# Retention states of both directions formed a head ahead, scores two steps ahead, five side banks

## The chip, the cores and the metric

The kernel runs on one core of a Trainium2 chip. The metric is the device time of one execution in microseconds (us), median of several runs. A core has a matrix engine (TensorE, in the profile PE, with its weight loads shown apart as PEld), a vector engine (VectorE, DVE), an engine for activations (ScalarE, ACT), a general one (GpSimd, POOL) and a queue that issues transfers (SyncE, SP). TensorE writes to PSUM, an accumulator of eight banks of 128 x 512 fp32 numbers.

## The reference, cut to what matters

The model is one layer of a diffusion transformer over 1024 latent tokens and 256 context tokens: a combined projection, retention and differential attention side by side, an output projection, and a gated feed-forward part. The change touches retention alone. It has four heads of 128 x 128, and it works in chunks of 128 tokens, in both directions over the sequence:

```python
def step(S, inp):                       # for each of 8 chunks; S starts from the context's 2 chunks
    qc, kc, vc = inp
    scores = einsum('bhid,bhjd->bhij', qc, kc) * intra
    o = einsum('bhij,bhje->bhie', scores, vc) + einsum('bhid,bhde->bhie', qc * q_dec[..., None], S)
    S = S * c_dec[:, None, None] + einsum('bhjd,bhje->bhde', kc * k_dec[..., None], vc)
    return S, o
...
for d in range(2):                      # forward, and backward over the flipped sequence
    o_l, _ = retention_chunked(ql, kl, vl, log_gamma[d], s_c)
    ret_lat = ret_lat + head_group_norm(orient(o_l), gn_g[d])
y_ret_lat = silu(rg_l) * ret_lat
```

So the state S of a chunk needs the state of the chunk before it, and each output needs one state of each direction.

## The kernel before, in words

Projections are done in fp32 split into a high and a low part, three matmuls of 512 columns for each product (`passes`, L129 to L131). A projection block is eight accumulations into a PSUM bank; each takes eight products (`KD`), 24 matmuls. `natural` (L387) and `transposed` (L442) run such blocks, and after each product they call `tick` (L376), which adds a rate to a counter and runs as many parts of a generator as the counter has whole numbers. Retention hangs on these ticks as side work. All of its matmuls are 128 x 128 in plain fp32, and the profile records two for each.

The parts around the change, in program order:

- The block of k (`transposed`, L695), which also writes k, transposed back, to DRAM.
- The block of the gate (`natural`, L698; 64 ticks). Beside it runs `states_before` (L318): the backward states of all four heads, 36 parts, one chunk each. GpSimd scales k (`kscale`, L229), TensorE forms k times v (`pub`, L334), VectorE adds it to the decayed state (`state_step`, L234), into `Sb`.
- The block of q (`transposed`, L701; 64 ticks), then six of the eight accumulations of the attention's q (L704; 48 ticks). Beside both runs `outputs` (L351) at 1.2 parts for each tick, from a counter of -12. A step is one chunk of one head; there are 32 steps, and each has three parts: the load and the score of the next step with the transpose of three steps back; the step's output; and the forward state's update with the gate of the step before.
- The last two accumulations of that block (L823), in whose course the attention begins.

In a step, `Step` has GpSimd scale q for both directions (`qq`, L256); `score` (L270) forms `pc` on TensorE and VectorE multiplies it with the decays (`sc`, L274); `output` (L276) accumulates `po` from four matmuls, ScalarE copies it to `o` (L282, two buffers) and sums its squares (L286), VectorE adds the norm's constant (`ss`, L114) and GpSimd raises to the power -1/2 (`ss`, L115); `update` (L289) forms `puf` and the next forward state `Sf`; `gate` (L295) multiplies with the norm on VectorE (L297) and adds and gates on GpSimd (`y`, L299, L300); `turn` (L302) transposes on TensorE (`pyt`, L304) and splits on ScalarE and VectorE (`yr`, L309, L310). The first forward state of a head comes from the context (`first_state`, L258; `context_keys`, L345, scaled by L348).

PSUM: the projections rotate through five banks (`mm_tiles`, L162), all side work through three (`pst`, L158, tag `tr`).

The order of the instructions of each engine is fixed when the kernel is built, by the framework: program order is the priority, but an instruction that by the framework's own estimate is not ready yet lets later ones go first. In the trace a product's three matmuls are therefore parted by side work at places. On the chip each engine then runs its list strictly in order.

Of the kernel before, what the change touches and what calls it, by code (L numbers as in the profile page):

```python
# [72 lines left out]
def kernel(  # L73
# [78 lines left out]
    with ExitStack() as p1:  # L152
# [8 lines left out]
        ps_b = psx.enter_context(tc.tile_pool(name="psb1", bufs=3, space=PSUM))  # L161
        mm_tiles = itertools.cycle([ps_b] * 3 + [ps_a] * 2)  # L162

        def mm_tile(name):
            return next(mm_tiles).tile([P, 512], F32, name=name, tag="mm")
# [52 lines left out]
        def load_kvg(h, g, nm, n, bufs=4):  # L218
            kvg = rt.tile([P, 2 if nm == "c" else 3, 2, P], F32, name=f"kvg{nm}", bufs=bufs)
            nc.sync.dma_start(out=kvg[:, :n], in_=kvg_d[g][:, :n, :, h * P : (h + 1) * P])  # L220
            return kvg
# [6 lines left out]

        def kscale(k1, h, d):  # L229
            kk = rt.tile([P, P], F32, name=f"ks{d}")  # L230
            nc.gpsimd.tensor_scalar(out=kk, in0=k1, scalar1=kd[:, h, d : d + 1], scalar2=0.0, op0=ALU.mult, op1=ALU.add)
            return kk

        def state_step(dst, prev, pu, h, d):  # L234
            if prev is None:
                nc.vector.tensor_copy(dst, pu)
            else:
                nc.vector.scalar_tensor_tensor(out=dst, in0=prev, scalar=cd[:, d * H + h : d * H + h + 1], in1=pu, op0=ALU.mult, op1=ALU.add)

        class Step:  # L240
            def __init__(self, n):
                self.h, self.t = divmod(n, NT)
                h, t = self.h, self.t
                if t % 2 == 0:
# [3 lines left out]
                    steps["pair"] = (qk, load_kvg(h, t // 2 + 1, "f", 3))  # L248
                qk, kvg = steps["pair"]
                self.qT, self.kT = (qk[:, i, t % 2 * P : (t % 2 + 1) * P] for i in range(2))  # L250
                self.kn, self.v, self.sg = (kvg[:, i, t % 2, :] for i in range(3))
                self.S = None
# [3 lines left out]
                nc.gpsimd.tensor_tensor(out=self.qq, in0=self.qT.unsqueeze(1).to_broadcast([P, 2, P]), in1=qd[:, h], op=ALU.mult)  # L256

            def first_state(self):  # L258
                ctx, kk = steps["ctx"]
                pu = pst.tile([P, NTC, P], F32, name="puc", tag="tr")  # L260
                for c in range(NTC):
                    mm(pu[:, c, :], kk[:, c, :], ctx[:, 1, c, :], start=True, stop=True)
# [55 lines left out]
        def states_before():  # L318
# [4 lines left out]
            for h, c in seq + [(None, None)]:  # L323
# [18 lines left out]
                if c is not None:  # L342
                    yield
# [7 lines left out]
        def outputs():  # L351
            n_steps = H * NT
            for n in range(-2, n_steps + 4):
# [12 lines left out]
                if new and (n + 1) % NT == 0:  # L366
                    steps[n + 1].first_state()
# [1011 lines left out]
```

## Time and profile before

| | |
|---|---|
| median of 3 runs | 1448.55 us (1448.17 to 1450.31) |
| the profiled execution | 1441.0 us, its span 1439.2 us |
| mean granted TensorE clock in it | 0.992 |
| PE, PEld busy | 1379.9 us (96%), 1141.9 us (79%) |
| DVE, ACT, POOL busy | 1003.8 us (70%), 732.4 us (51%), 340.8 us (24%) |
| chain that ended last | PE 66%, DVE 8%, DMA 5%, POOL 3% |

Durations come from the profiled execution. A line of the profile names the engine, the line of the kernel, the tiles (what is written, an arrow, what is read), the shapes and the count. Behind the bar stand busy time and the mean of one instruction in ns, then the idle time of the engine just ahead of it with what ended it. A matmul's end is modelled, so the start of the next one says more than its recorded duration. A waiting weight load (PEld) is the first sign of TensorE standing still.

### The profile page before, as it was taken

The numbers are of one execution on the slowest core, as the hardware profiler recorded it, in microseconds if no ns is written. First come the engines' busy times: TensorE is split into PE (matmuls) and PEld (weight loads), VectorE is DVE, ScalarE is ACT, GpSimd is POOL, SyncE is SP. The second block draws the span as 40 slices with busy tenths as digits, with TensorE's granted clock in tenths as the row PEclk, the third lists the DMA queues.
The fourth block names the chain that finished last, engine by engine and source line by source line (L and its number), as shares of the span: only waits on it lengthen the run. The fifth ranks groups of instructions, "written<-read, shape, count | busy, mean of one in ns | idle before, by whom it ended". The sixth has DMA issues, their size and how long they took to land.

```text
span 1439.2 us, 19420 instructions
## 1 busy us (share of the span) xinstructions
PE 1379.9 (96%) x6924; PEld 1141.9 (79%) x6924; DVE 1003.8 (70%) x1493; ACT 732.4 (51%) x1394; POOL 340.8 (24%) x451
## 2 busy tenths in 40 slices
PE   6999999999899899999999899999999999999996
PEld 2678787887777789999888677888888888888885
DVE  3565655333677598888346888878777777998457
ACT  3535512322456688998224655555555545455533
POOL 1210000022787323431002253322223230000001
PEclk9999999999999999999999999999999999999999
DMA  8557655466455767480511123223222224953224
GB/s 332 199 194 240 219 196 190 137 193 195 134 173 164 208 156 164 121 143 1 220 62 78 59 104 118 108 110 110 92 87 93 110 110 174 391 206 102 101 95 176
DMA packets 107673, 218.30 MB, mean 152 GB/s; under 512 B 8948, under 2 KB 47348, under 8 KB 106680
## 3 DMA queue, kind: packets, MB, share of 16 engines
q1 hardware_dynamic: 99448, 192.14, 38.3%
q0 software_dynamic: 8128, 24.91, 7.7%
q8 instruction: 55, 0.90, 0.3%
q14 instruction: 42, 0.34, 0.1%
HBM read 159.61 MB, written 57.41 MB: 151 GB/s over the span
## 4 chain that ended last, share of the span: by engine, by line
PE 66%; DVE 8%; DMA 5%; POOL 3%; issue 3%; ACT 3%; SPq 0%; POOLq 0%; DVEq 0%; ACTq 0%
PE chain L129 5%; PE pv L760 5%; PE chain L130 5%; PE pA L728 5%; PE chain L131 5%; PE c L131 4%; PE c L129 4%; PE c L130 4%; PE third L130 2%; PE third L129 2%; PE third L131 2%; DMA W<-w_down 2%; PE pt L748 2%; PE pn L130 2%; PE pn L131 2%
## 5 line engine op out<-in xcount | busy, mean ns | idle before, releaser
L129 PE MATMUL chain<-T,whi 128*128 128x512 f32 x264 | 103.8, 394 | 4.9 <-ACT T L941 3.3
L129 PE MATMUL pl<-hT,whi 128*128 128x512 f32 x256 | 107.1, 419 | 0.0
L130 PE MATMUL chain<-T,whi 128*128 128x512 f32 x264 | 103.2, 391 | 0.0
L131 PE MATMUL chain<-T,wlo 128*128 128x512 f32 x264 | 102.6, 390 | 0.0
L131 PE MATMUL pl<-hT,wlo 128*128 128x512 f32 x256 | 100.5, 393 | 0.0
L130 PE MATMUL pl<-hT,whi 128*128 128x512 f32 x256 | 100.5, 393 | 0.0
L731 DVE TENSOR_REDUCE mt<-pA 128x1 f32<-128x1280 f32 x64 | 95.3, 1490 | 3.3 <-PE pA L728 1.5
L728 PE MATMUL pA<-ks,qhl 128*128 128x512 f32 (+1 forms) x384 | 91.6, 375 | 4.7 <-ACT p L735 4.7
L1024 POOL TENSOR_TENSOR cmb<-wrb 128x512 f32<-128x512 f32 x22 | 36.2, 1647 | 243.2 <-DMA wrb<-w_up 141.3
L131 PE MATMUL c<-whi,ghl 128*128 128x512 f32 x232 | 90.4, 390 | 0.2 <-DVE ghl L1183 0.2
L130 PE MATMUL c<-wlo,ghl 128*128 128x512 f32 x232 | 90.3, 389 | 0.0
L129 PE MATMUL c<-whi,ghl 128*128 128x512 f32 x232 | 90.2, 389 | 0.0
L115 POOL TENSOR_TENSOR sm<-sm,mhalf 128x1 f32<-128x1 f32 x26 | 16.1, 621 | 304.7 <-DVE sm L114 301.4
L735 ACT ACTIVATE p<-pA,mt 128x1280 f32<-128x1280 f32 x64 | 85.5, 1336 | 4.6 <-DVE mt L731 4.5
L894 ACT CAST whi<-cmb 128x512 fp32r<-128x512 f32 x66 | 41.0, 622 | 83.5 <-PE chain L130 63.7
L728 PEld LDWEIGHTS pA<-ks,qhl 128*128 128x128 f32 x384 | 68.9, 193 | 17.5 <-ACT p L735 5.8
L129 PE MATMUL pn<-whi,hT 128*128 128x512 f32 x192 | 79.1, 412 | 0.0
L760 PE MATMUL pv<-va,aT 128*128 128x128 f32 x640 | 77.0, 275 | 0.1
L131 PE MATMUL pn<-whi,hT 128*128 128x512 f32 x192 | 75.9, 398 | 0.5 <-DVE hT L540 0.5
L130 PE MATMUL pn<-wlo,hT 128*128 128x512 f32 x192 | 76.1, 396 | 0.0
L895 DVE TENSOR_TENSOR wlo<-cmb,whi 128x512 fp32r<-128x512 f32 x66 | 60.7, 922 | 20.2 <-ACT whi L894 20.2
L760 PEld LDWEIGHTS pv<-va,aT 128*128 128x128 f32 x640 | 74.0, 192 | 0.7 <-DVE yT L789 0.3
(301 smaller groups left out, 3884.1 us busy)
## 6 DMA issues: line engine op xcount, KB each, us to landing
wm<-w_mod SPq DMA_DIRECT2D x32, 512.0 KB, 4.4
raw<-w_in SPq DMA_DIRECT2D x28, 512.0 KB, 4.4
wra<-w_up SPq DMA_DIRECT2D x24, 512.0 KB, 3.2
wrb<-w_up SPq DMA_DIRECT2D x24, 512.0 KB, 3.5
W<-w_down SPq DMA_DIRECT2D x44, 256.0 KB, 6.4
ad<-s SPq DMA_DIRECT2D x20, 512.0 KB, 3.4
wra<-ad SPq DMA_DIRECT2D x20, 512.0 KB, 3.2
wrb<-ad SPq DMA_DIRECT2D x18, 512.0 KB, 3.3
```

The lines of the kernel that those rows point to most:

```text
L115: nc.gpsimd.tensor_tensor(out=out_ap, in0=out_ap, in1=mhalf[:, :n], op=ALU.pow)
L129: mm(ps, lh, rh, start=first, stop=False, skip_group_check=more)
L130: mm(ps, lh, rl, start=False, stop=False, skip_group_check=more)
L131: mm(ps, ll, rh, start=False, stop=last, skip_group_check=more)
L728: mm(self.pa[m][:, c0:c1], self.q[:, i, m, qs], self.k[:, m, c0:c1], start=(i == 0), stop=(i == 1))
L731: nc.vector.tensor_reduce(out=self.mt[:, m : m + 1], in_=self.pa[m][:, :LK], axis=AX.X, op=ALU.min)
L735: nc.scalar.activation(self.p[m], self.pa[m][:, :LK], AF.Exp, scale=-1.0, bias=self.mt[:, m : m + 1], accum_out=self.s[:, m : m + 1])
L748: nc.tensor.transpose(self.pt[g][:, i, :], self.p[0][:, (4 * g + i) * P : (4 * g + i + 1) * P], ident)
L760: mm(self.pv, self.aT[:, c, :], self.v[:, c, :], start=(c == 0), stop=(c == NKT - 1))
L894: nc.scalar.copy(hi, src)
L895: nc.vector.tensor_tensor(out=lo, in0=src, in1=r32(hi), op=ALU.subtract)
L1024: nc.gpsimd.tensor_tensor(out=s1, in0=b1, in1=b2, op=ALU.add)
```

## The change

States of both directions are formed by one generator, `states(h)`: pairs of chunks are loaded (`kvs`, four buffers), GpSimd scales both chunks of a pair in one instruction (`ks`, 128 x 256), and forward and backward pairs alternate; a head has 18 parts as before (9 for each direction). The states of heads 0 and 1 are formed beside the gate's block, those of heads 2 and 3 within `outputs`, from steps 8 and 16 on, three parts in each of the first six steps of the head. All states lie in `S0` and `S1`, with buffers for two heads. `update`, `first_state`, `context_keys` and their tiles are gone. A step loads v and gate alone (`kvo`) and q and k.

The score is formed two steps ahead of the output instead of one (`lead = 2`; `qq` and `sc` get three buffers). Parts of a step: score with transpose; output with gate; in steps outside 8 to 23 an empty part. The rate is 1.5 for each tick from -21. The norm's constant is added on GpSimd (`tensor_scalar`), just ahead of the power.

From the gate's block on, the banks are dealt anew: three for the projections, five for the side work.

```diff
-        ps_b = psx.enter_context(tc.tile_pool(name="psb1", bufs=3, space=PSUM))
-        mm_tiles = itertools.cycle([ps_b] * 3 + [ps_a] * 2)
+        psbS = psx.enter_context(ExitStack())
+        ps_b = psbS.enter_context(tc.tile_pool(name="psb1", bufs=3, space=PSUM))
+        banks = dict(mm=itertools.cycle([ps_b] * 3 + [ps_a] * 2))
...
+        def tr_tile(shape, name):
+            return next(banks["tr"]).tile(shape, F32, name=name, tag="tr")
...
+        def load_kv(h, g, nm, s0, bufs):
+            kv = rt.tile([P, 2, 2, P], F32, name=nm, bufs=bufs)
+            nc.sync.dma_start(out=kv, in_=kvg_d[g][:, s0 : s0 + 2, :, h * P : (h + 1) * P])
+            return kv
...
-                    steps["pair"] = (qk, load_kvg(h, t // 2 + 1, "f", 3))
+                    steps["pair"] = (qk, load_kv(h, t // 2 + 1, "kvo", 1, 3))
...
-                if t < NT - 1:
-                    self.kk = kscale(self.kn, h, 0)
-                self.qq = rt.tile([P, 2, P], F32, name="qq")
+                self.qq = rt.tile([P, 2, P], F32, name="qq", bufs=3)
...
-                self.sc = rt.tile([P, 2, P], F32, name="sc")
+                self.sc = rt.tile([P, 2, P], F32, name="sc", bufs=3)
...
-                for d, Sd in enumerate((self.S, Sbs[self.h][:, self.t, :])):
+                for d in range(2):
                     mm(po[:, d, :], self.sc[:, d, :], self.v, start=True, stop=False)
-                    mm(po[:, d, :], self.qq[:, d, :], Sd, start=False, stop=True)
+                    mm(po[:, d, :], self.qq[:, d, :], before[self.h][d][:, self.t, :], start=False, stop=True)
...
-                rsqrt(self.ss, self.ss, 1.0, GN_EPS * P, 2)
+                nc.gpsimd.tensor_scalar(out=self.ss, in0=self.ss, scalar1=1.0, scalar2=GN_EPS * P, op0=ALU.mult, op1=ALU.add)
+                nc.gpsimd.tensor_tensor(out=self.ss, in0=self.ss, in1=mhalf[:, :2], op=ALU.pow)
...
+        def states(h):
+            seq = [(0, 0, (0, 1)), (1, 0, (1, 0))]
+            for g in range(1, 5):
+                seq += [(0, g, (0, 1) if g < 4 else (0,)), (1, 5 - g, (1, 0) if g < 4 else (1,))]
+            before[h] = [rt.tile([P, NT, P], F32, name=f"S{d}") for d in range(2)]
...
+            def loaded(i):
+                d, g, cs = seq[i]
+                kv = ctx if i == 1 else load_kv(h, g, "kvs", 0, 4)
+                ks = rt.tile([P, 2, P], F32, name="ks")
+                nc.gpsimd.tensor_scalar(out=ks, in0=kv[:, 0], scalar1=kd[:, h, d : d + 1], scalar2=0.0, op0=ALU.mult, op1=ALU.add)
+                return kv, ks
...
+            for i, (d, g, cs) in enumerate(seq):
+                kv, ks = ahead
+                if i + 1 < len(seq):
+                    ahead = loaded(i + 1)
+                for c in cs:
+                    pu = tr_tile([P, P], "pu")
+                    mm(pu, ks[:, c, :], kv[:, 1, c, :], start=True, stop=True)
...
+                    last[d] = dst
+                    yield
...
         def outputs():
             n_steps = H * NT
-            for n in range(-2, n_steps + 4):
-                new = 0 <= n + 1 < n_steps
-                if new:
-                    steps[n + 1] = Step(n + 1)
-                    steps[n + 1].score()
+            lead = 2
+            more = iter(())
+            for n in range(-lead, n_steps + 4):
+                if n + lead < n_steps:
+                    steps[n + lead] = Step(n + lead)
+                    steps[n + lead].score()
                 if 0 <= n - 3 < n_steps:
                     steps[n - 3].turn()
                 yield
                 if 0 <= n < n_steps:
                     steps[n].output()
-                yield
-                if 0 <= n < n_steps and n % NT < NT - 1:
-                    steps[n].update(steps[n + 1])
...
+                if n == NT:
+                    more = states(2)
+                if n == 2 * NT:
+                    more = states(3)
                 if 0 <= n - 1 < n_steps:
                     steps[n - 1].gate()
                 yield
+                if not NT <= n < 3 * NT:
+                    yield
+                for _ in range(3 if n % NT < 6 else 0):
+                    if next(more, more) is None:
+                        yield
...
         wg = stream_block(3)
+        psbS.close()
+        psb2 = psx.enter_context(ExitStack())
+        tr2 = psb2.enter_context(tc.tile_pool(name="tr2", bufs=2, space=PSUM))
+        mm2 = psb2.enter_context(tc.tile_pool(name="mm2", bufs=1, space=PSUM))
+        banks.update(mm=itertools.cycle([ps_a, ps_a, mm2]), tr=itertools.cycle([pst] * 3 + [tr2] * 2))
         beside(states_before(), 36 / 62)
...
-        beside(outputs(), 1.2, -12.0)
+        beside(outputs(), 1.5, -21.0)
...
         psx.close()
+        banks["mm"] = itertools.repeat(ps_a)
```

More of the change, by code (lines that the diff above doesn't have):

```diff
@@ L253, in __init__ @@
[L253 to L268 removed]
+                self.v, self.sg = (kv[:, i, t % 2, :] for i in range(2))
@@ L302, in turn @@
             def turn(self):
[L303 removed]
+                pt = tr_tile([P, P], "pyt")
                 nc.tensor.transpose(pt, self.y, ident)
```

84 lines of the change are left out of this document (18 added, 66 removed).

## The prediction, made before the changed kernel ran

> **What bounds the kernel now.** I read the page first, then the stages around the change, then TensorE's two lists in the stretch where the steps run.
>
> ```profile
> span 1439.2 us, 19420 instructions
> PE 1379.9 (96%) x6924; PEld 1141.9 (79%) x6924; DVE 1003.8 (70%) x1493; ACT 732.4 (51%) x1394; POOL 340.8 (24%) x451
> ```
>
> TensorE is busy for 96% of the span: what does not shorten its work or its standing still gains nothing. The change removes none of its work, since each head forms 18 states before and after. So only standing time can be won.
>
> ```profile
> core 0: us, PE busy (x) PEld busy (x) DVE busy (x) ACT busy (x) POOL busy (x), PEclk, DMA share, GB/s
> 288.00:342.00 54.00, 53.34 (x270) 44.25 (x269) 18.29 (x42) 11.57 (x16) 15.21 (x36) 1.00 0.61 185
> 342.00:358.00 16.00, 14.27 (x63) 11.28 (x62) 6.76 (x9) 5.08 (x7) 0.00 (x0) 1.00 0.67 217
> 358.00:478.00 120.00, 109.58 (x668) 92.00 (x669) 84.55 (x229) 65.39 (x226) 94.03 (x157) 1.00 0.48 154
> 478.00:497.00 19.00, 19.00 (x86) 15.72 (x85) 10.53 (x17) 10.56 (x18) 6.03 (x9) 1.00 0.95 228
> ```
>
> These are the gate's block (288 to 342 us), the q block before the first step's data is there (to 358), the 32 steps (to 478), and the projection that runs on alone afterwards. In the first stage TensorE lacks 0.66 us of 54, so nothing is to be had there. From 342 to 478 it lacks 1.73 + 10.42 = 12.15 us of 136. GpSimd is busy for 94 of the 120 us of the steps, 78%, against 24% over the span. The clock is 1.00.
>
> Matmul ends are modelled, so I count again from starts, in the window 342 to 478:
>
> ```profile
> L129 PE MATMUL pl<-hT,whi 128*128 128x512 f32 x102 | 46.2, 453 | 0.0
> L279 PEld LDWEIGHTS po<-kvgf,sc 128*128 128x128 f32 x128 | 20.8, 190 | 12.3 <-DVE Sf L238 9.4 <-DVE sc L274 0.9
> L280 PEld LDWEIGHTS po<-Sf,qq 128*128 128x128 f32 x64 | 9.8, 191 | 0.4 <-POOL qq L256 0.4
> L272 PEld LDWEIGHTS pc<-qk 128*128 128x128 f32 x64 | 10.6, 190 | 4.2 <-DMA qk<-rqk 2.6 <-DVE yr L310 0.2
> L291 PEld LDWEIGHTS puf<-kvgf,ks 128*128 128x128 f32 x56 | 9.9, 188 | 4.4 <-DVE sc L274 1.9 <-issue 0.6 <-POOL y L299 0.2
> L304 PEld LDWEIGHTS pyt<-ident,y 128*128 128x128 f32 x32 | 4.5, 142 | 3.6 <-POOL y L300 2.9 <-issue 0.3
> L262 PEld LDWEIGHTS puc<-kvgc 128*128 128x128 f32 x16 | 2.2, 190 | 1.0 <-DVE sc L274 0.9
> ...
> 342.79 0.40 PE L129 MATMUL pl<-hT,whi 128*128 128x512 f32 x1
> 355.88 0.39 PE L129 MATMUL pl<-hT,whi 128*128 128x512 f32 x1
> ...
> 360.96 0.39 PE L279 MATMUL po<-kvgf,sc 128*128 128x128 f32 x2
> 362.52 0.39 PE L291 MATMUL puf<-kvgf,ks 128*128 128x128 f32 x2
> ```
>
> Between the two projection rows lie 19 products of three matmuls without a break: 13.09 / 57 = 0.230 us each. Between the last two rows lie seven fp32 pairs back to back: 1.56 / 7 = 0.223 us a pair. A product has three matmuls, so the window holds 3 x 102 = 306, or 70.4 us. The fp32 matmuls are 128 + 64 + 64 + 64 + 56 + 16 = 392 records (po counts a second row like the one of L280, for `Sb`), 196 pairs, 43.7 us. The 32 transposes, one record each, take half a pair: 3.6 us. That makes 117.7 of 136 us: TensorE stands for about 18.3 us, half again what the busy column shows. The weight loads' waits name the causes, 19.4 us in sum, which I scale by 18.3 / 19.4 = 0.94: the forward state (9.4) 8.9; the scores `sc` (0.9 + 1.9 + 0.9) 3.5; `y` on GpSimd (2.9 + 0.2) 2.9; the first load of q (2.6) 2.5; the rest 0.5.
>
> **The change part by part.** *States a head ahead.* A step no longer waits for the state that was formed just before it, and no longer for the bank that this state's `puf` holds: five banks and states ready a head earlier take away both. Gain 8.9 us. Matmuls and state steps stay at 72 each. In the gate's block 36 parts with 20 loads become 36 parts with 18 loads, 36 instructions on GpSimd become 20, and VectorE's chain alternates between two directions: nothing.
>
> *Scores two steps ahead.* Every `sc` gets a step more before it is needed, so the 3.5 us go. VectorE stands in its list for the power:
>
> ```profile
> DVE o L297 <- POOL ss L115: 19.6, 21, 1.7
> ```
>
> The longest such wait, 1.7 us, holds up what is queued behind it (`sc`, the state step, the split of `yr`, the projection's rotation). One step more is at least 2.6 us (below), so `sc` is covered; if it is not, 3.5 us come back.
>
> *GpSimd.* Here is the price. The steps of heads 0 and 3 become dense: three parts at 1.5 for each tick make 2 ticks a step, against 2.5 before (three parts at 1.2). TensorE needs 6 x 0.230 for two products, 5 x 0.223 for `pc` and `po`, and 0.11 for the transpose: 2.61 us a step. GpSimd needs for the same step:
>
> ```profile
> L256 POOL TENSOR_TENSOR qq<-qk,qd 128x256 f32<-128x256 f32 x32 | 27.0, 845 | 19.5 <-DMA qk<-rqk 16.8 <-PE po L280 2.0 <-POOL ks L231 0.5
> L115 POOL TENSOR_TENSOR ss<-ss,mhalf 128x2 f32<-128x2 f32 x32 | 23.9, 748 | 2.5 <-DVE ss L114 2.0
> L300 POOL TENSOR_TENSOR y<-y,kvgf 128x128 f32<-128x128 f32 x32 | 16.0, 500 | 1.9
> L299 POOL TENSOR_TENSOR y<-o 128x128 f32<-128x128 f32 x32 | 15.6, 487 | 17.0 <-DVE o L297 17.0
> ...
> L256 POOL TENSOR_TENSOR qq<-qk,qd x32: 727/740/1702, 358.5 to 467.3; 128x256 f32<-128x256 f32 x32
> L115 POOL TENSOR_TENSOR ss<-ss,mhalf x32: 689/698/1142, 363.7 to 475.0; 128x2 f32<-128x2 f32 x32
> ...
> L771 POOL TENSOR_TENSOR e<-sa x32: 184/190/213, 503.3 to 686.1; 128x1 f32<-128x1 f32 x32
> L231 POOL TENSOR_SCALAR ks<-kvgf,kd x26: 368/377/1407, 360.8 to 464.2; 128x128 f32<-128x128 f32 x26
> L348 POOL TENSOR_SCALAR kvgc<-kvgc,kd x4: 481/483/1043, 262.2 to 418.6; 128x256 f32<-128x256 f32 x4
> ```
>
> The means give 0.845 + 0.748 + 0.500 + 0.487 = 2.58 us. The norm's constant on 128 x 2 is not in this trace on GpSimd: not below the 0.19 of the smallest two-input instruction, not above the power's 0.75. The same kind at 128 and 256 columns, 0.377 and 0.483, leads to about 0.27 at none; I take 0.25. A dense step then costs GpSimd 2.83 us; with medians for the first two and 0.19 it is 2.61, with 0.75 it is 3.33. There are 16 dense steps: 16 x (2.83 - 2.61) = 3.5 us of new standing, from 0 to 11.5. In heads 1 and 2 a step takes 34 parts / 1.5 / 8 = 2.83 ticks: 1.95 + 1.23 + 18/8 x 0.223 = 3.68 us on TensorE, and on GpSimd 2.83 + 10/8 x 0.48 = 3.43: covered. The forward `ks` of before (377) go.
>
> The same price from the other side, the chain of one step from `o` to `y`:
>
> ```profile
> 361.66 0.37 ACT L282 COPY o<-po 128x256 f32<-128x256 f32 x1 [7.10 <-PE po L280]
> 365.26 0.46 POOL L299 TENSOR_TENSOR y<-o 128x128 f32<-128x128 f32 x1 [0.48 <-DVE o L297]
> ...
> 402.04 0.38 PE L279 MATMUL po<-kvgf,sc 128*128 128x128 f32 x2
> 403.18 0.37 ACT L282 COPY o<-po 128x256 f32<-128x256 f32 x1 [1.38 <-POOL ks L231]
> 410.13 0.45 POOL L299 TENSOR_TENSOR y<-o 128x128 f32<-128x128 f32 x1
> ...
> 472.96 0.37 ACT L282 COPY o<-po 128x256 f32<-128x256 f32 x1 [1.37 <-PE po L280]
> 476.44 0.46 POOL L299 TENSOR_TENSOR y<-o 128x128 f32<-128x128 f32 x1 [0.79 <-DVE o L297]
> ```
>
> From the copy to the end of the sum it is 4.1 us in the first step, 3.9 in the last, 7.4 at the longest; over all 32 the mean is 5.2. The transpose of step n stands in TensorE's list five ticks, 2.5 steps, behind its output: 6.5 us in a dense step. It needs 1.1 (output to copy) + 5.2 + 0.5 (the second GpSimd instruction) = 6.8. So the pace would be 6.8 / 2.5 = 2.7 us, and 16 x 0.1 = 1.8 us. The two prices lie over each other, they do not add; I keep 3.5.
>
> *Transfers.* In the steps 16 loads of 384 KB become 16 of 256 KB, and 18 of 256 KB for the states take the place of the context's three or four.
>
> ```profile
> kvgf<-kvg SPq DMA_DIRECT2D x16, 256.0 KB, 2.9
> ```
>
> A pair of chunks lasts two parts, 1.3 ticks, over 1 us, and four buffers give SP's issues more than 3 us ahead: a load of 2.9 us is just covered. If not, GpSimd stands in its `ks` ahead of `qq` and the power. The first load of q still ends on the same chain, so its 2.5 us stay.
>
> *Banks.* The projections keep three instead of five.
>
> ```profile
> 479.94 2.39 ACT L420 ACTIVATE xb<-pl 32x512 f32<-32x512 f32 x4 [0.38 <-PE pl L131]
> ```
>
> Reading a bank takes ScalarE 2.4 us and VectorE one instruction more; two other accumulations of 24 x 0.230 = 5.5 us lie between. Nothing.
>
> *End.* The last transpose falls on tick 100 instead of 101, and 19 us of projection alone still follow, which cover the loads of the attention.
>
> Sum: -8.9 - 3.5 + 3.5 = -8.9 us. The profiled execution of 1441.0 would become 1432.1; it lies 7.6 us under the median of the runs, and the difference goes onto the median: 1448.55 - 8.9 = 1439.7.
>
> **The rivals.** *GpSimd held by VectorE* (no change). Some GpSimd instructions run long where VectorE works on two operands from SBUF:
>
> ```profile
> 394.00 1.29 POOL L256 TENSOR_TENSOR qq<-qk,qd 128x256 f32<-128x256 f32 x1
> 394.01 0.69 DVE L424 TENSOR_TENSOR xb<-xb,rtab 128x512 f32<-128x512 f32 x1
> ...
> L297 DVE SCALAR_TENSOR_TENSOR o<-o,ss,gn x64: 333/350/830, 364.5 to 476.0; 128x128 f32<-128x128 f32 x64
> ```
>
> Here `qq` took 1.29 instead of 0.74. If both gate instructions (0.35 each, both operands in SBUF) held GpSimd in each dense step, it would need 2.61 + 0.70 = 3.31 us, 16 x 0.70 = 11.2 us: 1448.55 - 12.4 + 11.2 = 1447.4. The Trainium skill, SBUF — State Buffer, section "Who interferes with whom", states just this: a VectorE instruction with two SBUF inputs and a GpSimd instruction that reads SBUF exclude each other for a whole instruction. By that rule the time is the 1447.4 of this rival. The trace agrees for single instructions, as with the 1.29, but the means above exceed the medians by 0.10 and 0.05 only, so it is no rule for every step.
>
> *Two buffers of `o`* (slower). `o` of step n + 2 waits for `y` of step n, so the chain sets a pace of half its length. ScalarE adds the rotation's copies (2.4 us in a row, above) to this chain in head 3. At 5.2 us the pace is 2.6 and costs nothing; from 2 x (2.61 + 12.4 / 16) = 6.8 us on, everything is eaten up. At 7.4, the longest seen: 16 x (3.7 - 2.61) - 12.4 = +5.0, 1453.6. For it speaks that GpSimd, VectorE and ScalarE all get denser; against it that the constant skips one engine.
>
> *The wait moves to `sc`.* VectorE keeps standing for the power and delays the scores all the same: the 3.5 us stay, 1443.2. Against it stands 1.7 us against a step.
>
> *All is won.* Only the first load stays: 18.3 - 2.5 = 15.8, 1432.8.
>
> **How the numbers follow.** The forecast, 1436 to 1442: 0.46. All won: 0.10. The wait moves: 0.18. GpSimd held: 0.16. Two buffers: 0.10. A measurement of this kernel tells 0.2%, 2.9 us, from no change: the first three lie beyond it, 0.74 faster; the fourth is within, 0.16; the fifth is slower, 0.10. The range, 1434.5 to 1450.0, cuts off the far half of "all won" and most of the last case. The likeliest case's own range is 1436 to 1442.
>
> **What would show it.** Right: no wait of `po` for a state, at most 1 us for `sc`; steps of heads 0 and 3 about 2.8 us apart; GpSimd's constant at 0.2 to 0.3 us; the projection's end (497 now) some 9 us earlier, all later stages as long as before. Wrong: `pyt` or `po` waiting long for `y`, `qq` or `o`; GpSimd waiting for `kvs`; a gap where the banks change hands or where the attention begins.

## The result and the profile after

The changed kernel takes 1460.02 us (median of 6 runs, 1457.04 to 1463.02) against 1448.36 (6 runs, 1442.11 to 1450.31): a ratio of 1.0092, 95% interval 1.0073 to 1.0111. It is slower by about 0.9%; the forecast was 0.6% faster, and 1460 lies beyond the range. The profiled execution of before (1441.0) happens to lie below all these runs and that of after (1463.0) is the longest of its own, so the spans differ by more than the medians do.

The first lines of the page of after:

```profile
span 1461.2 us, 19419 instructions
PE 1389.5 (95%) x6924; PEld 1148.0 (79%) x6924; DVE 994.2 (68%) x1461; ACT 732.3 (50%) x1394; POOL 341.4 (23%) x455
```

The busy times say next to nothing: VectorE does a little less, ScalarE and GpSimd the same. So I cut the span at two marks, the first matmul of the gate's block and the last of the projection beside which the steps run. Timeline of TensorE, before (start, duration):

```profile
288.12 0.40 PE L129 MATMUL pn<-whi,hT 128*128 128x512 f32 x1
...
497.02 0.39 PE L131 MATMUL pl<-hT,wlo 128*128 128x512 f32 x1
```

and after:

```profile
296.80 0.39 PE L129 MATMUL pn<-whi,hT 128*128 128x512 f32 x1
...
518.38 0.39 PE L131 MATMUL pl<-hT,wlo 128*128 128x512 f32 x1
```

From mark to mark it is 208.9 us before and 221.6 after, 12.7 us more. Behind the second mark both need the same: 1439.2 - 497.0 = 942.2 and 1461.2 - 518.4 = 942.8. The 8.7 us ahead of the first mark belong to no part of the change: in the experiments below this mark lies anywhere from 287.1 to 296.5, whatever the kernel.

As in the prediction I counted TensorE's standing from starts: the distance from each matmul to the next, less what that pair of kinds usually takes, put down to the tile that starts late. Between the two marks (the last four columns are the tiles that start late; `pu` stands for `puf` too):

```
                       region   stands   po    pu   pyt    pc
before                  208.9     19.3   9.5   1.9   3.1   2.9
after                   221.6     31.4   4.4   9.1  12.2   4.3
```

The 5.1 us that `po` no longer stands are there, and far more came back at `pyt` (9.1) and at the states (7.2). The list of waits of after, for 342 to 505 us (what waited, for what; us in all, times, longest):

```profile
DVE o L271 <- POOL ss L267: 48.7, 32, 2.7
ACT o L261 <- POOL y L273: 19.7, 12, 3.3
POOL y L273 <- DVE o L271: 17.7, 25, 1.7
PEld pyt L278 <- POOL y L274: 13.5, 11, 2.9
PE pyt L278 <- POOL y L274: 10.2, 10, 2.4
PEld po L258 <- DVE S L321: 3.2, 2, 1.9
PEld po L258 <- DVE sc L253: 0.3, 1, 0.3
```

VectorE stands for the power at every step, 48.7 us against 19.6 before; ScalarE and TensorE stand for `y`. Three engines wait for GpSimd. What GpSimd does meanwhile shows its timeline in head 3 (duration second; in brackets how long it stood before, and for what):

```profile
475.16 0.19 POOL L266 TENSOR_SCALAR ss<-ss 128x2 f32<-128x2 f32 x1
475.43 0.70 POOL L267 TENSOR_TENSOR ss<-ss,mhalf 128x2 f32<-128x2 f32 x1
476.10 0.72 POOL L247 TENSOR_TENSOR qq<-qk,qd 128x256 f32<-128x256 f32 x1
477.31 0.46 POOL L273 TENSOR_TENSOR y<-o 128x128 f32<-128x128 f32 x1 [0.49 <-DVE o L271]
477.85 0.46 POOL L274 TENSOR_TENSOR y<-y,kvo 128x128 f32<-128x128 f32 x1
478.39 0.19 POOL L266 TENSOR_SCALAR ss<-ss 128x2 f32<-128x2 f32 x1
478.66 0.69 POOL L267 TENSOR_TENSOR ss<-ss,mhalf 128x2 f32<-128x2 f32 x1
480.08 0.47 POOL L273 TENSOR_TENSOR y<-o 128x128 f32<-128x128 f32 x1 [0.73 <-DVE o L271]
480.63 0.46 POOL L274 TENSOR_TENSOR y<-y,kvo 128x128 f32<-128x128 f32 x1
481.04 0.74 POOL L247 TENSOR_TENSOR qq<-qk,qd 128x256 f32<-128x256 f32 x1
481.87 0.19 POOL L266 TENSOR_SCALAR ss<-ss 128x2 f32<-128x2 f32 x1
```

In these rows it is never late for want of work. It does the constant and the power, then stands for VectorE's gate, because `y` of the same step is next in its list; then two times `y`, and the next constant follows 0.1 us behind. Nothing from another step fills the 0.5 to 0.7 us in which it stands. Two steps here are 3.2 and 3.5 us long (478.39 - 475.16, 481.87 - 478.39), where the prediction had TensorE at 2.61 and GpSimd at 2.83.

The starts of the power give the length of a step in each head. For steps 0, 8, 16, 24 and 31 they are 363.72, 391.62, 420.49, 450.65 and 474.96 us before, and 370.84, 400.13, 433.88, 471.83 and 495.28 after. A step of heads 0 to 3 took 3.5, 3.6, 3.8 and 3.5 us before; it takes 3.7, 4.2, 4.7 and 3.4 after. So the dense steps hardly changed, and the loss lies in heads 1 and 2, beside whose steps the states of heads 2 and 3 are now formed.

Over all steps, from the first power to the last `y`, the busy times of the stretch (columns as in the prediction's table of stages), before and after:

```profile
363.70:477.50 113.80, 103.87 (x628) 86.72 (x627) 81.19 (x222) 63.34 (x217) 90.33 (x151) 1.00 0.48 153
```

```profile
370.80:498.20 127.40, 106.27 (x632) 88.60 (x630) 75.44 (x195) 62.91 (x219) 96.44 (x173) 0.99 0.49 152
```

and GpSimd's groups in the stretch of after:

```profile
L247 POOL TENSOR_TENSOR qq<-qk,qd 128x256 f32<-128x256 f32 x28 | 24.0, 857 | 0.1
L267 POOL TENSOR_TENSOR ss<-ss,mhalf 128x2 f32<-128x2 f32 x32 | 22.3, 697 | 2.5
L274 POOL TENSOR_TENSOR y<-y,kvo 128x128 f32<-128x128 f32 x32 | 18.5, 580 | 2.1
L273 POOL TENSOR_TENSOR y<-o 128x128 f32<-128x128 f32 x32 | 15.8, 495 | 20.8 <-DVE o L271 17.7 <-PE pl L131 1.6 <-DMA kvo<-kvg 1.0
L304 POOL TENSOR_SCALAR ks<-kvs,kd 128x256 f32<-128x256 f32 x18 | 9.9, 551 | 2.0 <-DMA kvs<-kvg 1.7 <-PE pu L316 0.2
L266 POOL TENSOR_SCALAR ss<-ss 128x2 f32<-128x2 f32 x31 | 7.5, 241 | 3.4 <-ACT jk L265 0.8
```

Three things lie in GpSimd's list itself: busy time, the wait for the gate in its own step, and the gaps without a releaser. Before: 90.3 + 17.0 + 2.4 (0.5 ahead of the power, 1.9 ahead of the second `y`, rows in the prediction) = 109.7 of 113.8 us, 96%. After: 96.4 + 17.7 + 7.2 (2.5 + 2.1 + 2.6) = 121.3 of 127.4, 95%. The list was full already, and it grew by 11.6 us of the 13.6 by which the stretch did.

### The profile page after: what moved, and what is told of

Same layout as the page of the kernel before. It is cut to its first block, busy times and chain, and to the rows that moved or that the text cites. A ratio compares the mean times of both kernels' runs of the same rounds, so it can differ in the third digit from the quotient of the medians.

```text
span 1461.2 us, 19419 instructions
## 1 busy us (share of the span) xinstructions
PE 1389.5 (95%) x6924; PEld 1148.0 (79%) x6924; DVE 994.2 (68%) x1461; ACT 732.3 (50%) x1394; POOL 341.4 (23%) x455
## 4 chain that ended last, share of the span: by engine, by line
PE 66%; DVE 6%; DMA 6%; POOL 4%; issue 3%; ACT 2%; SPq 0%; POOLq 0%; DVEq 0%; ACTq 0%
PE chain L129 5%; PE pv L749 5%; PE pA L717 5%; PE chain L130 5%; PE chain L131 5%; PE c L131 4%; PE c L129 3%; PE c L130 3%; PE third L129 2%; PE third L130 2%; PE third L131 2%; PE pt L737 2%; PE pn L130 2%; PE pn L131 2%; PE pn L129 2%
## 5 line engine op out<-in xcount | busy, mean ns | idle before, releaser
L130 PE MATMUL c<-wlo,ghl 128*128 128x512 f32 x232 | 90.3, 389 | 0.0
L129 PE MATMUL c<-whi,ghl 128*128 128x512 f32 x232 | 90.3, 389 | 0.0
L403 ACT ACTIVATE xb<-pl 32x512 f32<-32x512 f32 (+1 forms) x96 | 56.8, 592 | 33.7 <-PE pl L131 32.3
```

Of the source, the lines that this page charges most:

```text
L129: mm(ps, lh, rh, start=first, stop=False, skip_group_check=more)
L130: mm(ps, lh, rl, start=False, stop=False, skip_group_check=more)
L403: nc.scalar.activation(xb[q * blk : (q + 1) * blk, :], pt[o : o + blk, :], AF.Copy, scale=scale)
```

## The experiments

Ratios are to the kernel before, run beside each on the same chip; with them the 95% interval. Regions and standing are counted as above, from one profiled execution each.

**The constant back on VectorE**, all else as in the changed kernel:

```diff
-                nc.gpsimd.tensor_scalar(out=self.ss, in0=self.ss, scalar1=1.0, scalar2=GN_EPS * P, op0=ALU.mult, op1=ALU.add)
+                nc.vector.tensor_scalar(out=self.ss, in0=self.ss, scalar1=1.0, scalar2=GN_EPS * P, op0=ALU.mult, op1=ALU.add)
```

> The changed kernel with the norm's constant back on VectorE, nothing else. Theory A (GpSimd's list is the pace: for each step it runs constant, power, waits for VectorE's gate, then two instructions for y, and takes the next step's constant only then): the list loses 0.24 us of work and the step to the power, about 0.3 to 0.5 us a step; over the 16 dense steps 5 to 8 us, so about 1453 against 1460 of the changed kernel and 1448.4 before. Theory B (two buffers of o set the pace): the chain from o to y keeps its length, at most 2 us: 1458 to 1461. Theory C (the uneven pace alone, dense in heads 0 and 3): nothing, 1460.

Measured: 1449.15 us, 1.0023 (1.0005 to 1.0041). Region 212.8, standing 22.9, of which `pyt` 7.2 and `pu` 7.5. The waits in its stretch, 342 to 505 us:

```profile
DVE o L271 <- POOL ss L267: 31.4, 29, 2.2
PE pyt L278 <- POOL y L274: 6.1, 6, 1.8
PEld po L258 <- DVE S L323: 1.3, 2, 1.0
```

Most of the loss is the constant: by the ratios about 10 us, more than the 5 to 8 expected. But without it the change is no gain either: the states hold up `po` for 2.5 us only (the 1.3 above, and 1.2 for the first state of a head), and `y` and `pu` hold up TensorE instead.

**`qq` on VectorE**, the constant stays on GpSimd:

```diff
-                nc.gpsimd.tensor_tensor(out=self.qq, in0=self.qT.unsqueeze(1)...
+                nc.vector.tensor_tensor(out=self.qq, in0=self.qT.unsqueeze(1)...
```

> The changed kernel with the scaling of q (qq) on VectorE instead of GpSimd, nothing else: GpSimd loses 0.74 to 0.84 us a step, 27 us in all, VectorE gets some 0.45 us a step. Theory A (GpSimd's list is the pace): a part of qq lies in the wait between power and y, so 0.3 to 0.6 us a step come back, over 32 steps 8 to 14 us: 1446 to 1452; the transpose's wait for y falls from 10 us to under 4. Theory B (two buffers of o): the chain o to y gets shorter only where it queues behind qq, 0 to 5 us. Theory D (VectorE is what holds the steps, since it stands 48.7 us for the power): it gets worse, 1462 to 1468.

Measured: 1444.88, 0.9999 (0.9981 to 1.0017). Region 210.5, 11.1 us shorter than that of the changed kernel: taking another instruction out of GpSimd's list does the same as taking out the constant. It may do more, since it is longer, but the two intervals overlap. The transpose's wait for `y` went from 10.2 to 6.5 us, not to under 4 as expected.

**More buffers**: four of `o` and `ss`, the transpose one step later, and three of the states' loads to make room.

```diff
-                self.o = rt.tile([P, 2, P], F32, name="o")
+                self.o = rt.tile([P, 2, P], F32, name="o", bufs=4)
...
-                self.ss = rt.tile([P, 2], F32, name="ss")
+                self.ss = rt.tile([P, 2], F32, name="ss", bufs=4)
...
-                if 0 <= n - 3 < n_steps:
-                    steps[n - 3].turn()
+                if 0 <= n - 4 < n_steps:
+                    steps[n - 4].turn()
...
-                kv = ctx if i == 1 else load_kv(h, g, "kvs", 0, 4)
+                kv = ctx if i == 1 else load_kv(h, g, "kvs", 0, 3)
```

> The changed kernel with four buffers of o and ss instead of two, the transpose four steps behind the output's step instead of three, and three buffers for the states' loads instead of four (for room). Theory B (two buffers of o and the place of the transpose are the pace): the waits of ScalarE for y (19.7 us) and of TensorE for y (10.2 us) go, 8 to 12 us: 1448 to 1452. Theory A (GpSimd's list is the pace): a later place only delays the wait, the first wait in each dense stretch is cushioned by one step (3 us), not the rate: 1455 to 1460.

Measured: 1459.22, 1.0091 (1.0069 to 1.0113), as slow as the change itself. ScalarE's 19.7 us of standing for `y` are gone from the list of waits, and the time is the same. The two buffers of `o` do not set the pace, nor does the transpose's place: the standing only moves (`pyt` 6.8, `po` 8.4, `pu` 11.7 of 32.1). One thing is not parted here: with a buffer less, GpSimd stands 7.3 us for the states' loads (1.7 in the changed kernel), which could hide a small gain.

**Another order of GpSimd's list**, on top of these buffers: `y` of a step is held behind the power of the next step, so that VectorE's gate runs beside that power.

```diff
-                nc.gpsimd.tensor_tensor(out=self.ss, in0=self.ss, in1=mhalf[:, :2], op=ALU.pow)
+                self.power = nc.gpsimd.tensor_tensor(out=self.ss, in0=self.ss, in1=mhalf[:, :2], op=ALU.pow)
...
-                nc.gpsimd.tensor_tensor(out=self.y, in0=self.o[:, 0, :], in1=self.o[:, 1, :], op=ALU.add)
+                added = nc.gpsimd.tensor_tensor(out=self.y, in0=self.o[:, 0, :], in1=self.o[:, 1, :], op=ALU.add)
+                later = steps.get(self.h * NT + self.t + 1)
+                if later is not None:
+                    tc.add_manual_dep(added.ins, later.power.ins.name, ..., reason="order")
```

> The kernel of e3_bufs with one thing more: GpSimd's list is told to run a step's constant and power ahead of the y of the step before, so that VectorE's gate runs beside them and GpSimd does not stand for it. Theory A: the wait between power and y (17.7 us in all, about 0.5 us a step) goes off GpSimd's list, and the time falls by 6 to 12 us against e3_bufs: 1445 to 1452. Theory B and C: no difference from e3_bufs. If GpSimd's plain busy time (2.8 us a dense step) is the pace, also none.

Measured: 1452.57, 1.0057 (1.0042 to 1.0072), 6.7 us less than with the buffers alone. GpSimd's groups, first with the buffers alone, then with the order (342 to 500 us; idle time behind the second bar):

```profile
L273 POOL TENSOR_TENSOR y<-o 128x128 f32<-128x128 f32 x32 | 15.8, 493 | 20.8 <-DVE o L271 18.3 <-PE pl L131 2.4
L304 POOL TENSOR_SCALAR ks<-kvs,kd 128x256 f32<-128x256 f32 x22 | 12.8, 583 | 8.6 <-DMA kvs<-kvg 7.3 <-PE pn L131 1.1
```

```profile
L273 POOL TENSOR_TENSOR y<-o 128x128 f32<-128x128 f32 x32 | 14.9, 466 | 0.3 <-DVE o L271 0.3
L307 POOL TENSOR_SCALAR ks<-kvs,kd 128x256 f32<-128x256 f32 x21 | 13.3, 636 | 18.1 <-DMA kvs<-kvg 14.7 <-PE pn L131 2.4 <-PE pl L131 1.1
```

The 18 us of waiting for the gate were real time of the list: they are gone, and about a third of them reach the end. The loads of the states, with one buffer less, take some of the rest (14.7 us of waiting, from 7.3).

**An even pace**, with the constant on VectorE: the side work's parts spread so that dense heads and heads with states take like time.

```diff
-                if not NT <= n < 3 * NT:
-                    yield
-                for _ in range(3 if n % NT < 6 else 0):
-                    if next(more, more) is None:
-                        yield
+                if not NT <= n < 3 * NT:
+                    yield
+                    if 0 <= n < n_steps:
+                        yield
+                else:
+                    for _ in range(3 if n % NT < 4 else 2):
+                        next(more, None)
+                        yield
...
-        beside(outputs(), 1.5, -21.0)
+        beside(outputs(), 1.72, -24.7)
```

> The kernel of e1_const_dve (changed kernel, constant on VectorE) with an even pace: heads 0 and 3 get a second empty part a step, the states' 18 parts spread over seven steps instead of six, rate 1.72 from -24.7, so a step takes 2.3 ticks in heads 0 and 3 (2.0 before) and 2.3 to 2.9 in heads 1 and 2 (1.3 to 3.3 before). Theory P (what e1 still has over the kernel before is the uneven pace: dense steps shorter than the norm's chain, so that the transposes wait for y): TensorE's standing for y falls from 7.2 us to under 3, the time to 1442 to 1445, under the kernel before (1446.1). Rival Q (the waits lie at the states: pu for its scaled k, the bank or the state before it): no gain, or a loss of up to 3 us.

Measured: 1447.85, 1.0016 (1.0000 to 1.0032). Against 1.0023 for the constant on VectorE alone nothing that could be told, and the 1442 to 1445 expected of an even pace did not come: `pyt` stands 4.7 instead of 7.2 us, `po` 6.2 instead of 2.6.

**Constant and `qq` both on VectorE**, in the changed kernel:

> The changed kernel with both the constant and qq on VectorE: GpSimd loses a further 0.24 us a step against e2, VectorE has all of it. Theory A (GpSimd's list is the pace): better than each alone, e1 1449.1 and e2 1444.9: 1438 to 1442. Rival D (by now VectorE, which stands in its list for the power, is the pace): no better than e2, 1444 to 1450.

Measured: 1444.95, 0.9998 (0.9983 to 1.0014), the same as with `qq` alone moved. The 1438 to 1442 expected from GpSimd's list did not come; it came out as the rival had it. Once `qq` is off GpSimd, the constant no longer counts there. So in the changed kernel GpSimd's list is the pace only up to this point; what holds the steps then was not settled.

**The kernel before, with the constant alone on GpSimd**, nothing else of the change:

```diff
-                rsqrt(self.ss, self.ss, 1.0, GN_EPS * P, 2)
+                nc.gpsimd.tensor_scalar(out=self.ss, in0=self.ss, scalar1=1.0, scalar2=GN_EPS * P, op0=ALU.mult, op1=ALU.add)
+                nc.gpsimd.tensor_tensor(out=self.ss, in0=self.ss, in1=mhalf[:, :2], op=ALU.pow)
```

> The kernel before with one part of the change alone: the norm's constant on GpSimd, ahead of the power. Theory A (a GpSimd list that already stands or works through the whole step gets 0.24 us of work more in its loop of power, gate and y): the cost shows here too; with 2.5 ticks a step (3.6 us with its waits) there is less need of it, so 2 to 6 us: 1448 to 1452. Rival (the constant costs only in the dense steps of the new order): within 1.5 us of before.

Measured: 1457.83, 1.0092 (1.0070 to 1.0114). This one line costs what the whole change costs, and over twice the 2 to 6 us expected of it. Region 222.4, standing 32.4 (`po` 11.6, `puf` 9.8). Two waits in its stretch:

```profile
DVE o L298 <- POOL ss L288: 43.5, 27, 3.2
PEld po L279 <- DVE Sf L238: 11.4, 12, 2.5
```

The wait for the forward state, 9.4 before, grew although nothing about the states was touched: VectorE stands longer for the power, and the state steps stand behind it in VectorE's list, most of them with work on the projection's tiles in between.

**The kernel before, with `qq` alone on VectorE** (the edit shown above):

> The kernel before with qq on VectorE, nothing of the change: GpSimd gets 27 us of work less, VectorE some 15 us more. Theory A: if GpSimd's list held the steps before as well (VectorE stood 19.6 us for the power, and behind it TensorE 9 us for the state), the time falls by 4 to 8 us: 1438 to 1442. Rival (before, the steps were bound by the state's own chain from TensorE to VectorE and back): within 1.5 us, or slower since VectorE carries more.

Measured: 1438.96, 0.9957 (0.9939 to 0.9975), quicker than both kernels. The same wait, and GpSimd's stretch from the first power to the last `y` with three of its groups:

```profile
PEld po L279 <- DVE Sf L238: 5.9, 9, 1.7
```

```profile
364.90:472.10 107.20, 102.96 (x634) 87.41 (x632) 85.07 (x251) 64.16 (x220) 72.34 (x123) 1.00 0.51 163
```

```profile
L115 POOL TENSOR_TENSOR ss<-ss,mhalf 128x2 f32<-128x2 f32 x32 | 23.7, 742 | 6.1 <-DVE ss L114 5.5
L299 POOL TENSOR_TENSOR y<-o 128x128 f32<-128x128 f32 x32 | 17.8, 557 | 20.0 <-DVE o L297 19.3 <-PE pl L131 0.8
L231 POOL TENSOR_SCALAR ks<-kvgf,kd 128x128 f32<-128x128 f32 x25 | 13.2, 528 | 5.0 <-PE puf L291 4.7
```

The wait for the state shrinks by 3.5 us without the states being moved. GpSimd now waits for others too, 5.5 us for the constant (2.0 before) and 4.7 for `puf`: 72.3 busy, 19.3 for the gate and 3.0 of gaps (0.6 ahead of the power, 2.4 ahead of the second `y`) fill 94.6 of 107.2 us, 88%.

**The constant on ScalarE**, in the kernel before:

```diff
-                rsqrt(self.ss, self.ss, 1.0, GN_EPS * P, 2)
+                nc.scalar.activation(self.ss, self.ss, AF.Copy, bias=GN_EPS * P)
+                nc.gpsimd.tensor_tensor(out=self.ss, in0=self.ss, in1=mhalf[:, :2], op=ALU.pow)
```

> The kernel before, with the norm's constant on ScalarE, right behind the squares that form its operand: GpSimd's list stays as it was, VectorE loses 32 instructions of 0.34 us and the 3.9 us that it stood in front of them. List theory (GpSimd's serial list sets the pace of the steps): the list is as long as before, only the power may start a little earlier: 1444 to 1449 us against 1448.4, VectorE's wait for the power stays at 14 to 20 us. Rival, VectorE is the pace, through what it does and stands for in its own list: 10.8 + 3.9 us go from VectorE and some 6 to 10 us from the time, 1438 to 1442.

Measured: 1444.21, 1.0000 (0.9979 to 1.0020). VectorE lost 32 instructions, and the time is the same: VectorE is not the pace. It stands 28.2 us for the power in place of 19.6 (14 to 20 were expected): what it no longer does, it waits.

**An instruction of no use on GpSimd**, in the kernel before, the constant staying on VectorE:

```diff
-                rsqrt(self.ss, self.ss, 1.0, GN_EPS * P, 2)
+                nc.vector.tensor_scalar(out=self.ss, in0=self.ss, scalar1=1.0, scalar2=GN_EPS * P, op0=ALU.mult, op1=ALU.add)
+                idle = rt.tile([P, 2], F32, name="idle")
+                nc.gpsimd.tensor_scalar(out=idle, in0=self.ss, scalar1=1.0, scalar2=GN_EPS * P, op0=ALU.mult, op1=ALU.add)
+                nc.gpsimd.tensor_tensor(out=self.ss, in0=self.ss, in1=mhalf[:, :2], op=ALU.pow)
```

> The kernel before, with the constant still on VectorE and one GpSimd instruction more for each step, 128 x 2, right ahead of the power, of which nobody uses the result. List theory: only the length of GpSimd's list counts, so it costs as much as the constant itself did, 32 times 0.27 to 0.41 us, 9 to 13 us: 1457 to 1461. Rival, the place of the constant in the chain: the constant costs on GpSimd because it can start only when GpSimd's list has come to it, while on VectorE it was done meanwhile; then an instruction without a use costs at most its length where GpSimd is the pace and mostly lies in the 17 us that GpSimd stands for VectorE: 1448 to 1452.

Measured: 1459.79, 1.0099 (1.0078 to 1.0121). Its stretch, and two of GpSimd's groups in it:

```profile
371.30:498.80 127.50, 109.20 (x626) 90.30 (x624) 82.22 (x221) 63.08 (x215) 97.72 (x182) 0.96 0.43 137
```

```profile
L302 POOL TENSOR_TENSOR y<-o 128x128 f32<-128x128 f32 x32 | 15.6, 486 | 18.6 <-DVE o L300 18.6
L289 POOL TENSOR_SCALAR idle<-ss 128x2 f32<-128x2 f32 x31 | 8.0, 258 | 4.8 <-DVE ss L287 2.5
```

0.26 us of work that nobody waits for make the kernel 14.8 us slower, 0.46 a step, while GpSimd is seen idle for 30 of these 127 us. So it is the length of its list, not the move of the constant from one engine to another. The useless instruction also stands between the constant and the power; but GpSimd stood for the constant only 2.5 us in all, so mostly its own list came last. The clock does not explain the price: it was 0.96 in this one stretch, but 0.988 on average over this kernel's runs, as over those of the kernel before beside it. It also costs more than its 0.26 us; the gap ahead of it (4.8 - 2.5 = 2.3 us, 0.07 each) makes 0.33 of it, the rest was not settled.

**The constant on ScalarE and `qq` on VectorE**, in the kernel before:

> The kernel before, with qq on VectorE and the constant on ScalarE. List theory: GpSimd's list is as short as in the kernel with qq on VectorE alone (1439.0), the power starts a little earlier: 1435 to 1440, and VectorE's wait for the power at most the 14 us of that kernel. Rival, VectorE is the pace now that it has qq: its 32 instructions less give 6 us or more, 1430 to 1434. If ScalarE's list becomes the pace (three instructions and two reads of accumulators in a row for each step, and the rotation's copies), 1441 or more.

Measured: 1440.66, 0.9964 (0.9949 to 0.9980), not told apart from `qq` alone. Region 201.9, standing 12.6. It lies just above the 1435 to 1440 expected, and VectorE stands 19.9 us for the power, where at most 14 were expected.

**The same two moves in the changed kernel:**

> The changed kernel, with qq on VectorE and the constant on ScalarE: everything else of the change (states a head ahead, scores two steps ahead, five banks for the steps and three for the projection) stays. It is to be set against the kernel before with the same two moves. If the rest of the change is worth the 12.4 us that the prediction counted once GpSimd is free, it is 5 us or more faster than that one, 1430 to 1434. If the wait for the state was itself made by GpSimd's list, it is as fast or slower, 1438 to 1445; the kernel with both on VectorE stood at 1445.0.

Measured: 1441.94, 0.9979 (0.9964 to 0.9995). Region 205.4, standing 15.5 (`pyt` 5.5, `pc` 4.1, `po` 2.8). With GpSimd relieved, the change's own parts are still worth nothing against 1440.66.

**The transpose one step later**, on this kernel, on the one before it, and on this one with the buffers of above:

> The changed kernel with qq on VectorE and the constant on ScalarE, and each transpose one step later in TensorE's list (n - 4 in place of n - 3). If the transposes' standing for y (5.5 of the 15.5 us that TensorE stands there) is all that hides the gain of the states ahead, the time falls by 4 to 5.5 us against 1441.9, to 1436.5 to 1438, and the transposes stand for at most 1 us. If the list behind it is the limit, the standing moves to the outputs and scores and the time stays within 2 us: 1440 to 1444.

> The kernel before with qq on VectorE and the constant on ScalarE, and each transpose one step later. Its transposes stood for 1.6 us only, its outputs 6.5 us, mostly for the forward state. A later transpose takes the 1.6 us at most: 1439 to 1441. Should it go to 1436 or below, the transposes held up the state's chain on VectorE too (the split of yr stands in the same list).

> As the first of these three, with four buffers of o and ss in place of two and three of the states' loads in place of four. If two buffers of o hold the chain once the transpose is later, another 2 us or more below the first; if not, the same within 1.5 us. Three buffers of loads may cost up to 2 us.

Measured: 1438.64, 0.9953 (0.9935 to 0.9970); 1437.67, 0.9948 (0.9931 to 0.9966); 1439.67, 0.9958 (0.9940 to 0.9975). In the changed kernel `pyt` stands 2.2 us instead of 5.5. Two waits of `pyt` without the later transpose (342 to 496 us, the groups of weight loads and of matmuls), and then with it (342 to 505 us):

```profile
L278 PEld LDWEIGHTS pyt<-ident,y 128*128 128x128 f32 x32 | 4.5, 142 | 6.7 <-POOL y L274 6.3 <-ACT o L261 0.3
L278 PE MATMUL pyt<-ident,y 128*128 128x128 f32 x32 | 9.2, 288 | 4.3 <-POOL y L274 4.0
```

```profile
PEld pyt L278 <- POOL y L274: 3.0, 3, 1.5
PE pyt L278 <- POOL y L274: 1.8, 2, 1.1
```

From 0.9979 to 0.9953 it gains somewhat less than the 4 to 5.5 us expected, and the intervals of the two touch; the region is 1.9 us shorter. But the kernel without the states ahead, at 0.9948, is as quick with the same edits. Moving the states gains nothing that can be told from here; the buffers do not either. In the kernel before, the later transpose may give more than the 1.6 us expected at most (0.9948 against 0.9964), but the intervals overlap. Five kernels lie from 0.9948 to 0.9964, and the intervals do not part them; the simplest is the one before with `qq` on VectorE (0.9957).

## Why the prediction was wrong, point by point

*What bounds the kernel.* TensorE's standing in the steps was counted right: 18.3 us there against 19.3 over the whole region. The causes were taken from the last releaser of each wait. That `po` waited for `Sf` was so; that its time would go with the move of the states was the error. VectorE's state step came late because of VectorE's own list: in none of the eight waits of the weight loads for a state (9.4 us) did the state step itself stand for `puf`. Ahead of it, but for the constant, stood in two of them (2.4 us) the gate that had waited for the power; in five (6.4 us) it was work on the projection's tiles, as here in the longest, where `po` stood 1.91 us until 425.47:

```profile
421.95 2.61 DVE L183 TENSOR_TENSOR wlo<-raw,whi 128x1024 fp32r<-128x1024 f32 x2
...
425.08 0.34 DVE L238 SCALAR_TENSOR_TENSOR Sf<-Sf,cd,puf 128x128 f32<-128x128 f32 x1
```

So the power, late because GpSimd's list was full, is only a part of this wait; how large a part was not settled. That GpSimd's list acts on it the experiments show. The useless instruction raised the standing of `po` from 9.5 to 15.3 us, `qq` on VectorE lowered it to 6.2 (same count), and neither touched a state.

*States a head ahead, 8.9 us; scores early, 3.5 us.* As mechanisms they came true: the loads of `po` wait 3.8 us for a state (3.2 for the first of a head, 0.6 for others), and 0.3 for `sc`. As gains they were nought: 1.0023 with the constant back on VectorE, and 1441.94 against 1440.66 with GpSimd relieved. More distance between producer and consumer makes no list shorter; TensorE stood for `y` and `pu` instead.

*GpSimd, 3.5 us.* This is the term that failed, and by far. A dense step was given 2.83 us of GpSimd: busy time alone. The row of L299 that the prediction quoted ended in "17.0 <-DVE o L297 17.0", and that was not charged, as if an idle engine could do other work. Here it didn't: the next entry of its list is the one that waits, and with the other order those 18 us went. With 17.0 / 32 = 0.53 us more, a dense step is 3.36 us, and a step of heads 1 and 2, "covered" at 3.43 against TensorE's 3.68, is 3.96. By the prediction's own way of summing, 16 x (3.36 - 2.61) + 16 x (3.96 - 3.68) = 12.0 + 4.5 = 16.5 us of new standing against 12.4 removed: 1452.7, slower, from rows that were on the table. If nothing of the 12.4 was to be had, as the experiments have it, the same sum gives 1448.55 + 16.5 = 1465.0; measured were 1460.0, between the two. That is nearness, not proof: the sum has 3.36 and 3.96 us where steps took 3.7 and 3.4, and 4.2 and 4.7. It still leaves out the gaps in GpSimd's list (7.2 us of the stretch) and its waits for other things, the loads among them (127.4 - 121.3 = 6.1 us), and it is far too small for heads 1 and 2.

*The constant's own length* was right. All 32 of them in after (least, middle, most):

```profile
L266 POOL TENSOR_SCALAR ss<-ss x32: 192/193/588, 370.6 to 495.0; 128x2 f32<-128x2 f32 x32
```

It is 0.24 us on average, 0.27 from its start to the power's in the timeline above. What it costs the kernel is 0.40 us a step: 1457.83 - 1445.01 = 12.8 us over 32.

*The other side of the same price*, the chain from `o` to `y` with the transpose 2.5 steps behind, pointed at the right victim, `pyt`, 12.2 us, but took the chain's length from before, where the list was shorter.

*The rivals.* "GpSimd held by VectorE" looked at the right engine, but for another cause, and forecast no change. The rule of the Trainium skill, SBUF — State Buffer, section "Who interferes with whom", which it drew on, shows in single instructions again. The constant took some 193 ns, but 350 to 588 in five of 32 cases, each time beside a VectorE instruction with two operands in SBUF. With `qq`, two operands in SBUF, on VectorE, the first `y` of a step went from 487 to 557 ns on average. That move still gained 6 us, so the rule is not what set the pace. "Two buffers of `o`", the only slower rival, foresaw the sign and the late `y` (ScalarE stands 19.7 us for it), but not the cause, so the sign was luck: four buffers leave 1459.22. "The wait moves to `sc`" and "all is won" did not come.

*What would show it wrong* was named rightly: "`pyt` or `po` waiting long for `y`".

The Trainium skill, Perfetto Trace Analysis, section "Identifying the Most-Contended Engine", has the bottleneck be the engine with the highest occupancy, and holds that for GpSimd the percentage is also a fair measure of how close it is to its limit. In the stretch of the steps the first agrees: before, GpSimd's 79% lie above VectorE's 71%, ScalarE's 56% and the 76% of TensorE's weight loads (for TensorE the page does not go by the matmul share), though over the whole span, at 24%, it is the least busy of all. The second does not agree as a measure of room: GpSimd was busy for 90.3 of 113.8 us, 79%, and 0.26 us more of work for each step came out at the end in full and more.

Not settled: why an instruction of 0.24 to 0.26 us costs 0.40 to 0.46 (a part of the 0.40 may be the clock, on average 0.986 over the runs with the constant alone on GpSimd and 0.988 over those of the kernel before beside them); what holds heads 1 and 2 of the changed kernel once GpSimd is relieved; and what could still be won of TensorE's 12.6 us of standing in the kernel before with both moves (6.5 of it still `po`, 2.6 `pc`, mostly the first load of q).

## What to carry to other kernels

For an engine that runs a list in order, charge each step with busy time plus every wait for something of the same step that stands in its list; if this sum fills the stretch, as here with 109.7 of 113.8 us, suspect the engine whatever its busy share. Here each of the two instructions added to it came out at the end. A wait's last releaser is only the next link: follow it (here `po` for the state, the state for VectorE's list, VectorE in part for the power, the power for GpSimd's list) before giving its time to a move that shortens no list. The cheapest test is an instruction of no use on the suspected engine; the cheapest remedy was to give its largest instruction to a neighbour (845 ns on GpSimd, 438 on VectorE).

## What the runs showed of the hardware

An operation on 128 x 2 numbers took GpSimd 0.19 us as a multiply with add, but 0.70 as a power, nearly as long as `qq` with 128 times the elements (all three are the middle of 32; `qq` 0.74). On VectorE `qq` took 0.44 us:

```profile
L256 DVE TENSOR_TENSOR qq<-qk,qd 128x256 f32<-128x256 f32 x32 | 14.0, 438 | 4.4 <-DMA qk<-rqk 2.3 <-PE po L280 2.1
```
